# A two-layer decoder trunk on one core: other places for loads, for one quarter of a sum, for operands of the first pair and for the last additions

## The chip, the cores and the metric

The kernel runs on one core of one Trainium2 chip. The core has five engines with queues of their own: TensorE (PE; its weight loads are listed as PEld), VectorE (DVE), ScalarE (ACT), GpSimd (POOL) and SyncE (SP). SP, ACT and POOL also issue DMAs. The metric is the time of one execution in device microseconds (us), the median of the runs. Lower is better.

## The reference

All arithmetic is in float32, for 512 tokens of width 1024 and two layers:

```python
def rms_norm(x, gain):
    inv = lax.rsqrt(jnp.mean(x * x, axis=-1, keepdims=True) + NORM_EPS)
    return (x * inv) * gain

def swiglu(h, w_gate, w_up, w_down):          # 1024 -> 2816 -> 1024
    return (jax.nn.silu(h @ w_gate) * (h @ w_up)) @ w_down

def reference(x, ...):
    for l in range(DEPTH):
        x = x + 0.5 * swiglu(rms_norm(x, ffn1_norm[l]), ffn1_wg[l], ffn1_wu[l], ffn1_wd[l])
        h = rms_norm(x, mix_norm[l])
        z = h @ w_in[l]                       # q, k, v and three parts of a short convolution
        attn_out = sliding_window_attention(q, k, v, attn_sink[l])
        conv_out = short_conv(conv_B, conv_C, conv_h, conv_w[l])
        x = x + jnp.concatenate([attn_out, conv_out], axis=-1) @ w_out[l]
        x = x + 0.5 * swiglu(rms_norm(x, ffn2_norm[l]), ffn2_wg[l], ffn2_wu[l], ffn2_wd[l])
    return rms_norm(x, final_norm)
```

## The kernel before, in words

**Precision.** Each operand is split in a high part (a cast by ACT, `wh`, `xh`) and a low part (the rest, a subtraction by DVE, `wl`, `xl`); `split` at L226 makes both. A product is three matmuls on PE: high by high, high by low, low by high.

**Layout.** Between the parts the sum x lies turned, channels on partitions, in eight tiles of 128 channels by 512 tokens. A feed-forward part runs through its stages in the order of `INNER`: two plain column blocks ("p") with their projection down ("d"), five pairs of column blocks ("w"), two shares of the down projection ("s") and a closing down projection of the last two blocks ("d", (9, 10)). The last part (`LAST`) ends in "e" instead and leaves its result with tokens on partitions.

**Seven products for eight.** A pair of column blocks, a share and the output projection of the mixing part multiply two-by-two block matrices with seven block products (`CHAINS`, steps 0 to 6). Their x-side operands are sums of blocks, b11, b21, t2, t3, t1, t4, b22, made by `Seven.make` with DVE additions and a split. Their weight sides a11, a12, s2, s3, s1, a22, s4 come from loads into ten raw tiles. In `need_split`, s2 is a DVE addition in place (L265), s4 another (L285), or a DMA that adds on its way. `winograd2` calls `norm.make` for the operands t1, t4 and b22 after steps 0, 1 and 2.

**Weights ahead.** `plan` lists all weight units in the order of use. `take_split` makes the split of a unit two units ahead (`SPLIT_AHEAD`), `need_raw` loads four units ahead (`LOAD_AHEAD`), all by SP's queue, into eight raw tiles. Loads that add to what has been loaded go by GpSimd's queue. So during the last share of a part the first units of the next part's weights are loaded already.

**Shares and their way back.** A share's results come out with tokens on partitions. `Apart` collects them in quarters (o, t): channel half o, token half t. `Apart.send` lets ACT lay the 16-bit halves apart (L141) and SP issue two transposing DMAs per quarter (L898). `Apart.back` lets ACT put a turned quarter together (two copies, L911) and DVE add it to x (two additions, L915). A quarter that was not sent is turned by PE (L921) and added at L926. In the second share of `INNER`, quarters (0,0), (1,1) and (1,0) are sent after steps 3, 4 and 5 (`SENT_AT`), and (1,1) is taken back after step 6. In the closing projection, whose output blocks c come in the order 4, 5, 6, 7, 0, 1, 2, 3, `BACK_AT` takes (0,0) and (0,1) back after c = 4 and (1,0) after c = 5. Each block is added to x (L1250), and `Norm.take` and `Norm.square` make the next part's operands from it: `xh` (ACT, L458), `xl` (DVE, L459) and squares (L464, L467, L468).

**Order.** A scheduler sets the order on each engine from the order of the code and its own estimates; `tc.issue_after(i)` puts what is traced in it behind instruction i on i's engine. The opening and the last block of the end are written out by hand (`tc.manual_schedule`).

**Opening.** x is loaded in pieces (`load_x(tp, c0, n)`: token pair tp, n channel tiles from c0) by SP and ACT, beside the first weights; PE runs spin products on zeros (`spin`) until they land, then turns x (`turn_x`) and begins the first three groups.

**End.** `Finale.last` finishes four token tiles. `close` adds the last product to y (DVE) and sums the squares (ACT); `guess` takes a reciprocal root (ACT), `mend` improves it by a Newton step (DVE, L433 to L435), `scale` multiplies and stores. For the last tile the columns come in two halves of 256, `one` and `two`.

Of the kernel before, what the change touches and what calls it, by code (L numbers as in the profile page):

```python
# [49 lines left out]


SENT_AT = {3: (0, 0), 4: (1, 1), 5: (1, 0)}
BACK_AT = {4: ((0, 0), (0, 1)), 5: ((1, 0),)}
FINAL_AT = {4: (), 5: (4, 5)}
STREAM_BACK_AT = {9: 0, 11: 1, 16: 2, 18: 3}
SCORES_AT = (5, 6, 7, 8, 9, 10, 12, 13)
# [19 lines left out]
def trunk_kernel(  # L76
# [117 lines left out]
    order = []  # L194
    raw_of, split_of = {}, {}
    roomy = set()
    state = {"raw": 0, "split": 0, "group": 0, "late": None}

    def add_unit(*unit):
        units.append(unit)  # L200
# [10 lines left out]
    def need_raw(u):  # L211

        while state["raw"] <= min(u, len(units) - 1):
            n = state["raw"]
            _, _, kc, _, wide = units[n][0]
            name, shape = f"raw_{n}", (P, kc, wide)
            r = form(name, F32, shape) if n in roomy else stock(name, shape=shape)
            if n >= OPEN:
                load(r, n, 0, kc)
            for more in units[n][1:]:  # L220
                nc.gpsimd.dma_start(out=r, in_=rows_of(*more), accum_op=ALU.add)  # L221
            raw_of[n] = r
            state["raw"] += 1
# [10 lines left out]
    def need_split(g):  # L234
        while state["split"] <= min(g, len(order) - 1):
# [1 line left out]
            u, what = order[n]  # L237
            far = what == "far"
            if what in (None, "far"):
                need_raw(u if far else u + LOAD_AHEAD)  # L240
                raw = raw_of.pop(u)
            elif isinstance(what, tuple) and what[0] == "end":

                _, what, h = what
                at = {"a11": 2, "s2": 2, "s3": 3, "s1": 3, "a12": 4, "a22": 5, "s4": 5}[what]
                need_raw(u + 3 * at + h + LOAD_AHEAD)
                raws = {name: u + 3 * i + h for i, name in enumerate(END_LOADS)}
                if what == "s2":
                    with tc.issue_after(state["rest"]):
                        nc.vector.tensor_add(raw_of[raws["a11"]], raw_of[raws["a11"]], raw_of[raws["s1"]])  # L250
                raw = raw_of[raws["a11" if what in ("s2", "s4") else what]]
            elif isinstance(what, tuple):

                what, h, how = what
                far = how == "far"
                last = {"a11": 0, "a12": 4, "s2": 2, "s3": 6, "s1": 2, "a22": 8, "s4": 4}[what]
                need_raw(u + h if far else u + max(last, 4) + h + LOAD_AHEAD)
                a11, s1, a12, s3, a22 = (raw_of.get(u + 2 * i + h) for i in range(5))
                if what == "s2":

                    late = state["late"] if h else None
                    if not state["late"] and how == "share":
                        late = state["rest"]
                    with tc.issue_after(late) if late else nullcontext():
                        nc.vector.tensor_add(a11, a11, s1)  # L265
                raw = {"a11": a11, "a12": a12, "s2": a11, "s3": s3, "s1": s1, "a22": a22, "s4": a12}[what]
# [3 lines left out]
            if far:  # L270
                sent = split_far(hi, lo, raw)
            else:
                state["cast"], state["rest"] = (i.ins for i in split(hi, lo, raw))
            if isinstance(order[n][1], tuple) and order[n][1][0] == "end":
                if what == "a12":
                    nc.gpsimd.dma_start(out=raw_of[raws["a11"]], in_=raw, accum_op=ALU.add)
# [81 lines left out]
    def plan():  # L358
# [19 lines left out]
        def ffn(wg, wu, wd, stages, near=False):  # L378
            for what, b in stages:
# [3 lines left out]
                if what == "w":  # L383
                    seven(
                        lambda o, j, h: ((wg, wu)[o], KC // 2 * j + 2 * h, 2, 2 * b * P, S),
                        lambda what, h: "far" if (b, what, h) == (1, "a11", 0) else None,
                    )
                if what == "s":
                    seven(
# [2 lines left out]
                    )  # L392
                if what == "d":
                    cols(wd, 2 * b[0], 2 * len(b), KC, how, len(b) == 2)
                if what == "e":
                    u = len(units)
                    roomy.update(range(u, u + 3))
# [235 lines left out]
    nc.vector.memset(warm, 0.0)  # L633
    nc.scalar.activation(warm, warm, AF.Abs_reciprocal_sqrt, bias=eps)
# [243 lines left out]
    class Apart:  # L878
# [14 lines left out]
        def send(self, o, t):  # L893

            to = self.sent[o, t] = g8(f"turned_{self.name}_{o}_{t}", U16, (P, 2, NT, H))
            for u in range(2):
                halves = lay_apart(self.y[2 * t + u, o], f"{self.name}_{o}_{2 * t + u}")
                nc.sync.dma_start_transpose(  # L898
                    to.rearrange("p a c s -> p (a c) s")[:, :, u * P : (u + 1) * P],
                    halves.rearrange("p a n -> p (a n)"),  # L900
                )

        def back(self, o, t):

# [27 lines left out]
    def ffn(norm, stages, after=None, late=None):  # L932
# [39 lines left out]
        def winograd2(b, between=None):  # L972
# [12 lines left out]
            for step, (acc, operand, start) in enumerate(CHAINS):  # L985
# [195 lines left out]
        for i, (what, b) in enumerate(stages):  # L1181
# [34 lines left out]
            elif what == "s":  # L1216

                def between(step):
# [21 lines left out]
            for c, acc in down(rhs, b == (0,), final):  # L1240
# [19 lines left out]
    class Finale:  # L1260
# [49 lines left out]
        def add(self, t, o, acc, by):  # L1310
            part = self.y[t][o]
            nc.vector.scalar_tensor_tensor(part, acc, by, part, op0=ALU.mult, op1=ALU.add)

        def close(self, acc, t, half, by, ssq, c0=0):

            wide = acc.shape[1]
            y = self.y[t][half][:, c0 : c0 + wide]
            nc.vector.scalar_tensor_tensor(y, acc, by, y, op0=ALU.mult, op1=ALU.add)
            sq = work.tile([P, S], F32, tag="nsq", bufs=2, name=f"ysq_{half}_{t}_{c0}")
            nc.scalar.activation(sq[:, :wide], y, AF.Square, accum_out=ssq)  # L1320

        def guess(self, t, ssq, rest):
            r = small(f"r_end{t}", 1)
            nc.scalar.activation(r, ssq, AF.Abs_reciprocal_sqrt, scale=1.0 / D, bias=rest)
            return r

        def mend(self, t, ssq, rest, r):
            v, y = (small(f"{n}_end{t}", 1) for n in "vy")
            nc.vector.scalar_tensor_tensor(v, ssq, 1.0 / D, rest, op0=ALU.mult, op1=ALU.add)
            newton(y, r, v)  # L1330
            return y

        def root(self, t, ssq, rest):

            return self.mend(t, ssq, rest, self.guess(t, ssq, rest))

        def last(self, ops, accs):

# [397 lines left out]
```

## Time and profile before

| | us |
|---|---|
| median of 3 runs | 1630.61 |
| lowest and highest run | 1630.34, 1632.09 |
| the profiled execution: its own time | 1632.9 |
| the profiled execution: span from first to last instruction | 1631.1 |
| PE busy | 1616.7 (99%) |
| DVE busy | 1368.8 (84%) |
| ACT busy | 1178.1 (72%) |
| HBM read | 264.29 MB, 163 GB/s over the span |

The rows of the profile below give a start and a length in us, the engine (with q: its queue, where DMAs are issued), the line, the operation, what is written and read, and the size. In brackets stands how long the engine was idle before it and what ended that. One product of 512 columns shows as 0.39 us long, but the next starts while it runs.

### The profile page before, as it was taken

To read this page: it belongs to the slowest core of one execution; us is meant where nothing else is said; L and a number is where in the kernel's file an instruction comes from. 1 tells how busy PE (TensorE), PEld (TensorE's weight loads), DVE (VectorE), ACT (ScalarE), POOL (GpSimd) and SP (SyncE) were. 2 spreads that over 40 slices of the span, in tenths; PEclk is the share of its full clock that TensorE was granted. 3 is DMA by queue.
4 is the path that set the end of the run, shared out by engine and by line. 5 is a ranking of instruction groups with operands and counts; after the bars stand their busy time and mean duration, and the time that the engine had idled before them with its cause. 6 is when DMAs were issued, how large, how long until landed. Compare 5 with 4: busy or idle time off the path is not lost.

```text
span 1631.1 us, 21176 instructions
## 1 busy us (share of the span) xinstructions
PE 1616.7 (99%) x7572; PEld 1348.1 (83%) x7572; DVE 1368.8 (84%) x1779; ACT 1178.1 (72%) x1510; POOL 223.6 (14%) x199
## 2 busy tenths in 40 slices
PE   9999999999999999999999999999999999999998
PEld 6788888878898888888888888888788988888887
DVE  7978797888899977797999777989788998677997
ACT  6667777867766577778865777787586767878665
POOL 1211111001121111111011111110012111111121
PEclk9999999999999999999999999999999999999999
DMA  9899989922597698999967999999135978999992
GB/s 271 198 237 212 210 210 239 242 68 73 129 238 180 178 217 213 214 213 247 228 143 188 217 215 219 214 237 221 52 91 152 233 152 215 225 220 231 240 250 71
DMA packets 307166, 318.12 MB, mean 195 GB/s; under 512 B 125612, under 2 KB 188660, under 8 KB 307060
## 3 DMA queue, kind: packets, MB, share of 16 engines
q1 hardware_dynamic: 265140, 230.63, 49.9%
q0 software_dynamic: 41200, 85.47, 30.5%
q8 instruction: 59, 0.97, 0.2%
q10 hardware_dynamic: 720, 0.66, 0.1%
q14 instruction: 47, 0.39, 0.1%
HBM read 264.29 MB, written 2.10 MB: 163 GB/s over the span
## 4 chain that ended last, share of the span: by engine, by line
PE 91%; DVE 5%; ACT 2%; DMA 1%; issue 1%; SPq 0%; ACTq 0%; DVEq 0%
PE x L824 26%; PE y L824 13%; PE x_s L824 9%; PE w L824 6%; PE acc L313 6%; PE acc L312 6%; PE acc L315 6%; PE y_s L824 5%; PE w_s L824 3%; PE x_m L809 3%; PE y_m L809 1%; DVE wl L226 1%; PE y_e L824 1%; PE acc L686 1%; PE x_e L824 1%
## 5 line engine op out<-in xcount | busy, mean ns | idle before, releaser
L226 DVE TENSOR_TENSOR wl<-raw,wh 128x1024 fp32r<-128x1024 f32 (+1 forms) x493 | 599.6, 1224 | 171.8 <-ACT wh L226 171.0
L226 ACT CAST wh<-raw 128x1024 fp32r<-128x1024 f32 (+1 forms) x493 | 513.9, 1046 | 302.2 <-PE x L824 95.0
L313 PE MATMUL acc<-xl,wh 128*128 128x512 f32 x392 | 153.6, 392 | 2.8 <-DVE xl L459 2.8
L312 PE MATMUL acc<-xh,wh 128*128 128x512 f32 x392 | 153.4, 393 | 0.5 <-ACT wh L226 0.5
L315 PE MATMUL acc<-xh,wl 128*128 128x512 f32 x384 | 149.6, 390 | 0.0
L221 POOL DMA_DIRECT2D raw<-in_ffn_wu_dram x40 | 50.2, 1264 | 386.1 <-DVE wl L226 203.8
L313 PEld LDWEIGHTS acc<-xl,wh 128*128 128x128 f32 x392 | 73.7, 188 | 18.7 <-DVE xl L459 4.4
L312 PEld LDWEIGHTS acc<-xh,wh 128*128 128x128 f32 x392 | 73.7, 188 | 15.5 <-ACT wh L226 0.6
L315 PEld LDWEIGHTS acc<-xh,wl 128*128 128x128 f32 x384 | 72.1, 188 | 15.0
L221 POOL DMA_DIRECT2D raw<-in_ffn_wg_dram x40 | 49.4, 1261 | 200.9 <-DMA raw<-in_ffn_wu_dram 82.9
L221 POOL DMA_DIRECT2D raw<-in_ffn_wd_dram x34 | 41.0, 1206 | 246.3 <-DMA raw<-in_ffn_wd_dram 109.7
L265 DVE TENSOR_TENSOR raw<-raw,raw 128x1024 f32<-128x1024 f32 x58 | 70.6, 1221 | 3.6 <-DMA raw<-in_ffn_wu_dram 3.2
L1086 ACT COPY raw_a<-turned 128x1024 uint16<-128x1024 uint16 x48 | 63.5, 1357 | 0.0
L824 PE MATMUL x<-wl,ft2h 128*128 128x512 f32 x160 | 62.2, 390 | 1.1 <-DVE wl L226 1.1
L824 PE MATMUL y<-wh,ft4h 128*128 128x512 f32 x160 | 62.4, 390 | 0.1
L824 PE MATMUL w<-wh,fb21h 128*128 128x512 f32 x160 | 62.3, 390 | 0.0
L824 PE MATMUL y<-wh,ft3h 128*128 128x512 f32 x160 | 62.3, 390 | 0.0
L824 PE MATMUL w<-wl,fb21h 128*128 128x512 f32 x160 | 62.3, 389 | 0.0
L824 PE MATMUL x<-wh,ft2h 128*128 128x512 f32 x160 | 62.3, 389 | 0.0
L824 PE MATMUL x<-wh,ft1h 128*128 128x512 f32 x160 | 62.3, 389 | 0.0
L824 PE MATMUL x<-wh,ft2l 128*128 128x512 f32 x160 | 62.3, 389 | 0.0
L824 PE MATMUL x<-wh,ft1l 128*128 128x512 f32 x160 | 62.3, 389 | 0.0
(506 smaller groups left out, 4545.2 us busy)
## 6 DMA issues: line engine op xcount, KB each, us to landing
raw<-in_ffn_wu_dram SPq DMA_DIRECT2D x127, 512.0 KB, 5.4
raw<-in_ffn_wd_dram SPq DMA_DIRECT2D x105, 512.0 KB, 5.8
raw<-in_ffn_wg_dram SPq DMA_DIRECT2D x86, 512.0 KB, 5.3
raw<-in_ffn_wu_dram POOLq DMA_DIRECT2D x40, 512.0 KB, 8.9
raw<-in_ffn_wg_dram POOLq DMA_DIRECT2D x40, 512.0 KB, 6.2
raw<-in_w_in_dram SPq DMA_DIRECT2D x36, 512.0 KB, 4.0
raw<-in_ffn_wd_dram POOLq DMA_DIRECT2D x34, 512.0 KB, 9.4
raw<-raw POOLq DMA_DIRECT2D x21, 512.0 KB, 7.9
```

The costliest lines, as they stand in the source:

```text
L221: nc.gpsimd.dma_start(out=r, in_=rows_of(*more), accum_op=ALU.add)
L226: return nc.scalar.copy(hi, raw), eng.tensor_sub(lo, raw, f32(hi))
L265: nc.vector.tensor_add(a11, a11, s1)
L312: nc.tensor.matmul(acc, hi[:, k, :], rhs[k][0], start=k == first, stop=False)
L313: nc.tensor.matmul(acc, hi[:, k, :], rhs[k][1], start=False, stop=False)
L315: nc.tensor.matmul(acc, lo[:, k, :], rhs[k][0], start=False, stop=k == last)
L686: nc.tensor.matmul(opening[n], (lo if part == "w" else hi)[:, k, :], xl if part == "x" else xh, start=n not in begun, stop=k == KC - 1 and ...
L809: nc.tensor.matmul(accs[c // 2][:, c % 2, :], w[:, k, cols], x_[:, 2 * h + k, :], start=start and c % 2 == 0 and h + k + i == 0, stop=h + ...
L824: nc.tensor.matmul(accs[u], x_[:, 2 * h + k, tok], w[:, k, :], start=start and h + k + i == 0, stop=h + k == 2 and i == 2, skip_group_chec ...
L1086: nc.scalar.copy(words(raws[self.b][:, c, :]), self.to[:, :, c, :])
```

## The change

Six edits:

1. **Loads held.** After step 0 of the second share, `need_raw` stops at the last unit of the closing projection (`closing`, `state["hold"]`). After c = 5 of the closing projection the hold is lifted, and the loads of the next part are put behind the last transposing DMA of the share on SP's queue (`state["behind"] = apart.last`), until c = 0.
2. **First quarter.** (0,0) is taken back after step 6 of the second share, ahead of (1,1), not after c = 4.
3. **First part's pairs.** In the first feed-forward part t1, t4 and b22 are made a step later, behind the latest weight split.
4. **Second pair of the first part.** The second addition for s2 is put behind the first split of a12.
5. **Opening.** Two spin products fall away; the piece (1, 1, 1) of x goes third on ACT's queue, and (0, 2, 2) goes on SP's.
6. **End.** For the last token tile the additions of both halves come ahead of what waits for the first half's squares, and the Newton step of the last root is written with one dependent step less.

On the engines this gives: PE runs the same products (the two spin products less), in four places of the first pair in another order; DVE, ACT and SP run the same number of instructions in another order; GpSimd's order is unchanged.

```diff
-BACK_AT = {4: ((0, 0), (0, 1)), 5: ((1, 0),)}
+BACK_AT = {4: ((0, 1),), 5: ((1, 0),)}
...
             if n >= OPEN:
-                load(r, n, 0, kc)
+                with tc.issue_after(state["behind"]) if state["behind"] else nullcontext():
+                    load(r, n, 0, kc)
...
-                need_raw(u if far else u + LOAD_AHEAD)
+                need_raw(u if far else max(u, min(u + LOAD_AHEAD, state["hold"] or len(units))))
...
+                    if how == "behind":
+                        late = state["mark"]
                     with tc.issue_after(late) if late else nullcontext():
                         nc.vector.tensor_add(a11, a11, s1)
...
+                if isinstance(order[n][1], tuple) and order[n][1][2] == "mark":
+                    state["mark"] = state["rest"]
...
-                        lambda what, h: "far" if (b, what, h) == (1, "a11", 0) else None,
+                        lambda what, h: "far"
+                        if (b, what, h) == (1, "a11", 0)
+                        else {("a12", 0): "mark", ("s2", 1): "behind"}.get((what, h))
+                        if near and b == 3
+                        else None,
...
                     cols(wd, 2 * b[0], 2 * len(b), KC, how, len(b) == 2)
+                    if len(b) == 2:
+                        closing.append(len(units) - 1)
...
-    load_x(0, 2, 2, nc.scalar)
-    load_x(1, 1, 1)
+    load_x(1, 1, 1, nc.scalar)
+    load_x(0, 2, 2)
...
         turn_rows(0)
-        spin(2)
         turn_x(0)
...
-                nc.sync.dma_start_transpose(
+                self.last = nc.sync.dma_start_transpose(
...
-                if step < 3:
-                    norm.make(CHAINS[step + 4][1])
+                due = step + (4 if norm.i else 3)
+                if 3 < due < len(CHAINS):
+                    with nullcontext() if norm.i else tc.issue_after(state["rest"]):
+                        norm.make(CHAINS[due][1])
...
+                    if step == 0:
+                        state["hold"] = closing[norm.i // 3 * 2 + norm.i % 3 // 2]
                     if step == 6:
+                        apart.back(0, 0)
                         apart.back(1, 1)
...
                 if final:
+                    if c == 5:
+                        state["hold"], state["behind"] = None, apart.last
+                    if c == 0:
+                        state["behind"] = None
...
                 early = self.guess(a, ssq, done[:, a : a + 1])
-                by = self.mend(a, ssq, done[:, a : a + 1], early)
+                v = self.mean(a, ssq, done[:, a : a + 1])
+                one = self.total(products(psum("mm", [P, H], "z_0"), 1, 0, H, True), b, 0, 0.5)
+                by = self.mend(a, v, early)
+                ssq = small("ssq_end_0", 1)
+                self.squared(one, ssq, "one")
                 for late in (0, 1):
                     scale(a, by, late)
-                one = piece(products(psum("mm", [P, H], "z_0"), 1, 0, H, True), b, 0, 0.5)
+                two = self.total(products(psum("mm", [P, H], "z_1"), 1, H, H, True), b, 0, 0.5, H)
                 rest = done[:, b : b + 1]
                 nc.vector.scalar_tensor_tensor(
-                    rest, one, 1.0 / D, rest, op0=ALU.mult, op1=ALU.add
+                    rest, ssq, 1.0 / D, rest, op0=ALU.mult, op1=ALU.add
                 )
-                two = piece(products(psum("mm", [P, H], "z_1"), 1, H, H, True), b, 0, 0.5, H)
-                by = self.mend(b, two, rest, self.guess(b, two, rest))
+                half = small("half", 1)
+                nc.vector.tensor_scalar_mul(half, rest, -0.5)
+                ssq, v, by = (small(f"{n}_last", 1) for n in ("ssq", "v", "y"))
+                self.squared(two, ssq, "two")
+                r = self.guess(b, ssq, rest)
+                nc.vector.scalar_tensor_tensor(v, ssq, -0.5 / D, half, op0=ALU.mult, op1=ALU.add)
+                nc.vector.tensor_scalar(v, v, r, r, op0=ALU.mult, op1=ALU.mult)
+                nc.vector.scalar_tensor_tensor(by, v, 1.5, r, op0=ALU.add, op1=ALU.mult)
```

Here `total` is the addition of the old `close`, `squared` its sum of squares, and `mean` the first step of the old `mend`.

More of the change, by code (lines that the diff above doesn't have):

```diff
@@ L196, in trunk_kernel @@
     roomy = set()
-    state = {"raw": 0, "split": 0, "group": 0, "late": None}
+    state = {"raw": 0, "split": 0, "group": 0, "late": None, "hold": None, "behind": None}
+    closing = []
     def add_unit(*unit):
@@ L897, in send @@
                 halves = lay_apart(self.y[2 * t + u, o], f"{self.name}_{o}_{2 * t + u}")
-                nc.sync.dma_start_transpose(
+                self.last = nc.sync.dma_start_transpose(
                     to.rearrange("p a c s -> p (a c) s")[:, :, u * P : (u + 1) * P],
                     halves.rearrange("p a n -> p (a n)"),
-                )
+                ).ins
         def back(self, o, t):
@@ L1312, in add, with total, squared @@
             nc.vector.scalar_tensor_tensor(part, acc, by, part, op0=ALU.mult, op1=ALU.add)
-        def close(self, acc, t, half, by, ssq, c0=0):
[L1316 to L1320, printed above, removed]
+        def total(self, acc, t, half, by, c0=0):
+            y = self.y[t][half][:, c0 : c0 + acc.shape[1]]
+            nc.vector.scalar_tensor_tensor(y, acc, by, y, op0=ALU.mult, op1=ALU.add)
+            return y
+        def squared(self, y, ssq, name):
+            sq = work.tile([P, S], F32, tag="nsq", bufs=2, name=f"ysq_{name}")
+            nc.scalar.activation(sq[:, : y.shape[1]], y, AF.Square, accum_out=ssq)
+        def close(self, acc, t, half, by, ssq, c0=0):
+            self.squared(self.total(acc, t, half, by, c0), ssq, f"{half}_{t}_{c0}")
         def guess(self, t, ssq, rest):
@@ L1325, in guess, with mean, mend @@
             return r
-        def mend(self, t, ssq, rest, r):
-            v, y = (small(f"{n}_end{t}", 1) for n in "vy")
+        def mean(self, t, ssq, rest):
+            v = small(f"v_end{t}", 1)
             nc.vector.scalar_tensor_tensor(v, ssq, 1.0 / D, rest, op0=ALU.mult, op1=ALU.add)
+            return v
+        def mend(self, t, v, r):
+            y = small(f"y_end{t}", 1)
             newton(y, r, v)
@@ L1333, in root @@
         def root(self, t, ssq, rest):
-            return self.mend(t, ssq, rest, self.guess(t, ssq, rest))
+            early = self.guess(t, ssq, rest)
+            return self.mend(t, self.mean(t, ssq, rest), early)
         def last(self, ops, accs):
```

## The prediction

> **What bounds the kernel now.** I read the page first, then what TensorE (PE) waited for, then the instructions in order of time at those places.
>
> ```profile
> span 1631.1 us, 21176 instructions
> PE 1616.7 (99%) x7572; PEld 1348.1 (83%) x7572; DVE 1368.8 (84%) x1779; ACT 1178.1 (72%) x1510; POOL 223.6 (14%) x199
> ```
>
> PE is busy for 99% of the span. A change that leaves PE's products alone, as this one does, can only win the time in which PE stood, at most 14.4 us. The waits of PE name who held it; the first figure is the total in us:
>
> ```profile
> PE acc L313 <- DVE xl L459: 2.8, 4, 1.1
> PE xt L652 <- DMA xin<-in_x_dram: 1.6, 1, 1.6
> ...
> PE x L824 <- DVE wl L226: 1.1, 1, 1.1
> ```
>
> Ends of products are modelled, so I price a stall by starts: 340.06 to 340.29 in the rows below is the undisturbed pace, 0.23 us a product.
>
> ```profile
> 56.73 0.39 PE L824 MATMUL x<-wh,ft2l 128*128 128x512 f32 x1
> ...
> 58.53 0.39 PE L824 MATMUL x<-wh,ft2h 128*128 128x512 f32 x1
> ...
> 68.98 0.39 PE L824 MATMUL x<-wh,ft1l 128*128 128x512 f32 x1
> ...
> 69.76 0.40 PE L824 MATMUL y<-wh,ft4l 128*128 128x512 f32 x1
> ...
> 340.06 0.40 PE L315 MATMUL acc<-xh,wl 128*128 128x512 f32 x1
> 340.29 0.40 PE L312 MATMUL acc<-xh,wh 128*128 128x512 f32 x1
> ...
> 343.35 0.39 PE L315 MATMUL acc<-xh,wl 128*128 128x512 f32 x1
> ...
> 1145.01 0.39 PE L315 MATMUL acc<-xh,wl 128*128 128x512 f32 x1
> ...
> 1148.60 0.40 PE L315 MATMUL acc<-xh,wl 128*128 128x512 f32 x1
> ```
>
> First pair of column blocks: 56.73 to 58.53 is two steps, 1.80 - 0.46 = 1.34 lost; 68.98 to 69.76 two steps, 0.32 lost; together 1.66. Entry of the mixing stage, layer 0: five steps in 3.06, 1.92 lost. Layer 1: six steps in 3.59, 2.21 lost. With the 1.58 us at 6.93 (below) and the tail after the last product these are the places the change touches.
>
> **The change part by part.** *Loads held back and first quarter sooner (three feed-forward ends).* Three like stretches, each from the closing projection into the next stage's first group; the columns are length, then busy time of PE, PEld, DVE, ACT:
>
> ```profile
> 320.00:343.00 23.00, 21.65 (x95) 17.27 (x93) 22.95 (x34) 17.96 (x24) 0.00 (x0) 1.00 0.57 159
> 802.50:825.50 23.00, 23.00 (x103) 19.07 (x102) 21.82 (x32) 16.98 (x25) 0.00 (x0) 1.00 0.47 148
> 1125.00:1148.20 23.20, 21.83 (x94) 17.22 (x93) 22.84 (x34) 17.99 (x24) 0.00 (x0) 1.00 0.57 159
> ```
>
> The middle one runs the same code without a PE stall, and there VectorE (DVE) has 1.2 us to spare. At the other two DVE is full: it entered late.
>
> ```profile
> 311.62 1.05 ACT L226 CAST wh<-raw 128x1024 fp32r<-128x1024 f32 x1
> 316.17 2.57 ACT L911 COPY back<-turned 128x1024 uint16<-128x1024 uint16 x2 [3.50 <-DMA turned<-halves]
> ...
> 313.84 1.28 DVE L891 SCALAR_TENSOR_TENSOR apart<-x_s,apart 128x512 f32<-128x512 f32 x2
> 317.55 0.69 DVE L915 TENSOR_TENSOR x<-x,back 128x512 f32<-128x512 f32 x1 [2.43 <-ACT back L911]
> ...
> 319.68 1.23 DVE L226 TENSOR_TENSOR wl<-raw,wh 128x1024 fp32r<-128x1024 f32 x1 [0.21 <-ACT wh L226]
> 320.82 0.68 DVE L1250 SCALAR_TENSOR_TENSOR x<-acc,x 128x512 f32<-128x512 f32 x1
> 321.42 1.42 DVE L915 TENSOR_TENSOR x<-x,back 128x512 f32<-128x512 f32 x2
> ```
>
> ScalarE (ACT) stands 3.50 us for transposes that lie behind two 512 KB loads in SP's queue, and DVE 2.43 us behind ACT. The order of the changed program puts the copies and additions of quarter (0,0), whose transposes went out a step earlier, in these holes, ahead of quarter (1,1): two ACT copies, 2.57 us together as in the 316.17 row, from 312.6 to 315.1, and the two additions, until now 1.42 us at 321.42, at about 315.0 and 315.7. The copies of (1,1) then start at 315.1 if their transposes are there (1.1 us sooner), so the weight cast after them, DVE's 319.68 row and everything behind it come 1.1 earlier, and from the place of the 321.42 row on 1.1 + 1.3 = 2.4 earlier. For no stall the two late low parts must come sooner by what PE lost up to the second, 1.8. So both stalls go: 1.92 + 2.21 = 4.13, taken as 4.1. At the middle boundary the inserted copies push ACT later by about 1.8 and DVE by 0.4; 1.2 us of spare covers it: nothing.
>
> What is moved to do this: on SP's queue two loads of 512 KB per boundary go behind four transposes and two more behind the last two of them. Nothing changes on GpSimd's queue.
>
> ```profile
> raw<-in_w_in_dram SPq DMA_DIRECT2D x36, 512.0 KB, 4.0
> 319.93 2.79 SPq L209 DMA_DIRECT2D raw<-in_w_in_dram  x3
> 329.50 1.04 ACT L226 CAST wh<-raw 128x1024 fp32r<-128x1024 f32 x1
> ```
>
> The first of these loads feeds the cast at 329.50, wanted at about 327.1. The last transposes end before 319.93 even in the old order; 4.0 us (median to landing) gives 323.9, and with a queue in front 325.3. Cost zero, covered by 2 to 3 us; without that cover each us is a us of DVE. Bounds of the whole part: 4.14 at most; at least 2.6, if the (1,1) transposes land no sooner (then only the 1.3 us of additions is won, against 1.8 wanted: 0.5 to 0.8 stays at each entry).
>
> *First pair's operands.*
>
> ```profile
> 51.24 1.22 DVE L592 TENSOR_TENSOR hf<-hf 128x1024 f32<-128x1024 f32 x1
> ...
> 54.65 1.22 DVE L226 TENSOR_TENSOR ft1l<-hf,ft1h 128x1024 fp32r<-128x1024 f32 x1
> ...
> 56.92 1.22 DVE L226 TENSOR_TENSOR wl<-raw,wh 128x1024 fp32r<-128x1024 f32 x1
> ```
>
> PE waits at 56.96 for the low weights made at 56.92. DVE is back to back here, one wide instruction each 1.13 us. The new order takes the 51.24 and 54.65 rows from in front of it: 2.27 sooner, 54.65, done 55.87. In the new PE order the third product of the step wants it, one pace ahead of the 56.73 row, at 56.50. Gone: 1.34. What is late next: t1's two DVE steps and its cast now come behind the third product's weights, and counting on at 1.13 a row the low weights of the t1 product are done at 67.28, wanted two steps of 24 products (0.2265 each) after 56.50, at 67.37. That cover is 0.1 thin, so I leave 0.1 of stall: gain 1.55, between 0.8 (0.8 late there) and 1.66. In the next pair one addition goes behind a split on DVE; PE waits for nothing there, and the loads behind it start about 2 us sooner: zero.
>
> *First loads and two spin products less.*
>
> ```profile
> 1.19 2.74 PE L151 MATMUL idle<-zero 128*128 128x512 bf16 x6 [1.19 <-DVE warm L633]
> 4.08 0.61 PE L151 MATMUL idle<-zero 128*128 128x512 bf16 x2
> ...
> 6.93 0.44 PE L652 MATMUL xt<-ident,xin 128*128 128x128 f32 x2 [1.58 <-DMA xin<-in_x_dram]
> ...
> 5.64 0.40 ACT L226 CAST wh<-raw 128x256 fp32r<-128x256 f32 x1 [1.28 <-DMA raw<-in_ffn_wg_dram]
> ...
> 8.46 0.42 ACT L226 CAST wh<-raw 128x256 fp32r<-128x256 f32 x1
> ```
>
> The x piece awaited at 6.93 is issued third on ACT's queue instead of fourth on SP's, ahead of 256 KB that went first. Then the first weight piece (5.64) leads, and after it the second weight piece, whose issue does not move: it followed the first by 1.56 us, so its cast could stand at 5.64 + 1.56 = 7.2 at the soonest against 8.46. Gain between -0.3 (the small piece delays the first weights) and 0.9; nearest is the 8.46 row, which had 0.46 of other ACT work in front and goes to 7.9 or 8.0. I take 0.55; PE then works without holes to 27.9, so it lasts.
> The clock is a risk: six spins take 2.74 us, 0.43 each, and the pair at 4.08 starts the second in 0.22. So PE was at full pace by 4.08, before the two that go. The Trainium skill, "TensorE: Matmul & The Clock Gate", Part 1, says that PE runs at half clock until a free-running window of about 3.4 us was busy, at a moment that varies by run. The two rows agree with half pace first; by that rule fewer spins could leave the opening cold, a rival below.
>
> *Last additions.*
>
> ```profile
> 1623.91 0.28 PE L1415 MATMUL z<-wl,fb_e 128*128 128x256 f32 x1
> 1623.71 0.42 DVE L1318 SCALAR_TENSOR_TENSOR ytok<-z,ytok 128x256 f32<-128x256 f32 x1
> ...
> 1624.78 0.42 DVE L1318 SCALAR_TENSOR_TENSOR ytok<-z,ytok 128x256 f32<-128x256 f32 x1
> ...
> 1626.10 0.16 DVE L433 TENSOR_TENSOR y_end<-r_end 128x1 f32<-128x1 f32 x1 [0.17 <-ACT r_end L1324]
> ...
> 1626.68 0.75 DVE L1364 SCALAR_TENSOR_TENSOR ytok<-ytok,y_end,gain 128x512 f32<-128x512 f32 x1
> ```
>
> The last product ends at 1624.19, but the last addition starts at 1624.78, because the sum of squares of the other half is waited for between. Now it starts at 1624.25: 0.53. After the root two dependent steps follow instead of three: 0.19 (1626.10 to 1626.68 is three). The extra small step lies beside ACT's squares. Sum 0.7, bounds 0.2 (order only in part) and 0.75.
>
> **Sum.** 4.1 + 1.55 + 0.55 + 0.7 = 6.9. The profiled execution took 1632.9, 2.3 above the median 1630.61 of the runs: 1626.0 by its own time, 1623.7 by the median.
>
> **Rivals.**
> 1. The transposes land no sooner: 0.5 + 0.8 stays at the entries, and 0.2 more of late weights: gain 5.4, 1625.2. Against it: the SP order no longer has the two loads in front.
> 2. Given back: PE enters mixing 2 us sooner, and there ACT and DVE set the pace of attention, so 2 us come back in each layer: gain 2.9, 1627.7. For it: DVE is 84% busy over all. Against it: DVE enters as much sooner, and the middle boundary goes on without a stall.
> 3. Cold opening: the 12 products and 12 transposes before 11.1 at half pace cost 12 x 0.2 + 12 x 0.1 = 3.6, of which about 1 fits in PE's holes: loss 2.6 for a gain of 0.55; 1626.9.
> 4. Slower: the held-back weights come late. A cast that stands blocks ACT, its split DVE, and PE's low parts queue behind. It decides when the first load lands after about 331, 11 us after the 319.93 row: then each of three boundaries loses over 2.3 us, 6.9 in all; at 332.5 it gives 1630.6 - 6.9 + 3 x 3.8 = 1635. Against it: 4.0 us to landing.
> 5. The change does not do what it says, 1630.6: only if the late steps stay late in the new order; the programs' order speaks against it.
>
> **How the numbers follow.** Forecast 0.62, rivals 0.15, 0.10, 0.05, 0.05, 0.03. A measurement of this kernel tells about 0.2%, 3.3 us, from no change. Rival 2 lies near that edge and is halved; of rival 3 0.04 is faster. Faster 0.62 + 0.15 + 0.05 + 0.04 = 0.86, same 0.05 + 0.01 + 0.03 = 0.09, slower 0.05. The bounds of the parts give gains from 3.3 (2.6 + 0.8 - 0.3 + 0.2) to 7.45, so 1627.3 to 1623.2; with the runs' spread, 1622.4 to 1627.5. The likeliest case alone: 1622.7 to 1624.7.
>
> **What would show it.** Right: no PE wait for xl at the two entries, and the (0,0) copies on ACT between 312 and 316; no PE wait at 58; products of the opening about 0.6 us sooner; the last addition right behind the last product. Wrong: a PE or ACT wait for DMA of the next stage's weights, a new PE wait for wl in the t1 product, 0.43 us between products after 6 us, or new PE waits in attention.

## The result and the profile after

| | before | after |
|---|---|---|
| median of 11 runs each | 1632.09 | 1627.79 |
| lowest and highest run | 1629.66, 1638.06 | 1626.69, 1629.26 |
| the profiled execution: its own time | 1632.9 | 1627.75 |
| the profiled execution: span | 1631.1 | 1626.0 |

The ratio is 0.9966, with a 95% interval of 0.9956 to 0.9976: the changed kernel is faster by 0.34% (0.24 to 0.44%), 4.3 us by the medians. The forecast of "faster" came true. The forecast time of 1623.7 did not: the measured 1627.79 lies 0.3 us above the top of the range. Part of that isn't the change: before's median in these 11 runs is 1.5 us above that of the 3 runs known earlier. Counted as a gain, 4.3 us came of the 6.9 forecast, inside the 3.1 to 8.2 that the range allowed.

The page of the changed kernel begins as before's did, with 3 us less of span at a PE that is as busy:

```profile
span 1626.0 us, 21171 instructions
...
PE 1616.4 (99%) x7570; PEld 1350.2 (83%) x7570; DVE 1367.4 (84%) x1779; ACT 1177.3 (72%) x1510; POOL 223.6 (14%) x199
```

**The entries of the mixing stage.** Here and below, a kernel's profile is that of one execution; before and the kernel called base below have two each. Two stretches of the changed kernel, one around each entry; the columns are length, then busy time of PE, PEld, DVE, ACT:

```profile
312.00:345.00 33.00, 33.00 (x151) 27.39 (x150) 30.28 (x43) 26.32 (x33) 0.00 (x0) 1.00 0.67 190
1120.00:1148.00 28.00, 28.00 (x125) 23.18 (x124) 25.79 (x36) 21.23 (x29) 0.00 (x0) 1.00 0.63 185
```

PE does not stand; the 1.92 and 2.21 us of before are gone. ACT, whose copies waited 3.50 us for the transposes, now does all four without a break in front of them, where the prediction put them. The two of quarter (1,1) are the last of the four and start at about 314.7, against 316.17 before:

```profile
312.29 5.00 ACT L922 COPY back<-turned 128x1024 uint16<-128x1024 uint16 x4
```

**The first pair.** Starts of PE's products in the changed kernel, first where t2 begins to be used, then at t1:

```profile
57.49 0.39 PE L835 MATMUL x<-wh,ft2h 128*128 128x512 f32 x1
57.72 0.39 PE L835 MATMUL x<-wh,ft2l 128*128 128x512 f32 x1
57.94 0.39 PE L835 MATMUL x<-wl,ft2h 128*128 128x512 f32 x1
...
68.82 0.48 PE L835 MATMUL x<-wl,ft1h 128*128 128x512 f32 x1
69.14 0.39 PE L835 MATMUL x<-wh,ft1h 128*128 128x512 f32 x1
```

The 1.34 us are gone, and of the 0.32 at t1 0.09 stays (0.32 between the last two rows, for 0.23). That is 1.57.

**The opening.** PE of the changed kernel, then the same core's stretches of 3.41 us; in a stretch the figure after the five engines is the granted clock:

```profile
5.67 0.44 PE L664 MATMUL xt<-ident,xin 128*128 128x128 f32 x2 [0.64 <-DMA xin<-in_x_dram]
6.87 0.50 PE L698 MATMUL acc<-xh,wh 128*128 128x512 f32 x1 [0.77 <-ACT xh L470]
...
9.53 0.63 PE L698 MATMUL acc<-xh,wl 128*128 128x512 f32 x1
9.96 0.63 PE L698 MATMUL acc<-xl,wh 128*128 128x512 f32 x1
...
29.36 0.26 PE L180 MATMUL par_ps<-ident,rows 56*128 56x56 f32 x1
```

```profile
4.28:7.69 3.41, 1.95 (x11) 1.04 (x10) 1.26 (x3) 1.70 (x5) 0.00 (x0) 1.00 1.00 310
7.69:11.10 3.41, 3.41 (x13) 2.83 (x13) 1.75 (x3) 1.52 (x3) 0.00 (x0) 0.50 0.99 338
11.10:14.51 3.41, 3.29 (x14) 2.10 (x13) 2.42 (x4) 3.14 (x8) 0.00 (x0) 1.00 1.13 349
```

The piece of x that before awaited until 6.93 is there at 5.67, and the first product starts at 6.87, not 7.13. Then PE gets half of its clock from 7.69 to 11.10, and its products come 0.43 us apart (9.53 to 9.96). The small product that ends the opening in the list above, the second transposes of the gains, stood in before at

```profile
27.92 0.26 PE L180 MATMUL par_ps<-ident,rows 56*128 56x56 f32 x1
```

So in these two executions the opening lost 1.44 us. I call the start of this product the end of the opening from here on.

**The end.** DVE, PE and ACT of the changed kernel behind the last product:

```profile
1619.44 0.28 PE L1447 MATMUL z<-wl,fb_e 128*128 128x256 f32 x1
```

```profile
1619.76 0.42 DVE L1337 SCALAR_TENSOR_TENSOR ytok<-z,ytok 128x256 f32<-128x256 f32 x1 [0.41 <-PE z L1447]
...
1621.09 0.27 DVE L1481 TENSOR_SCALAR v_last<-v_last,r_end 128x1 f32<-128x1 f32 x1 [0.17 <-ACT r_end L1351]
1621.39 0.16 DVE L1482 SCALAR_TENSOR_TENSOR y_last<-v_last,r_end 128x1 f32<-128x1 f32 x1
1621.59 0.75 DVE L1396 SCALAR_TENSOR_TENSOR ytok<-ytok,y_last,gain 128x512 f32<-128x512 f32 x1
```

The last addition starts 0.32 us after the last product's start (0.87 before): 0.55 won. From it to the last scaling are 1.83 us (1.90 before): 0.07 won.

The sum of the two profiles: + 1.44 - 1.57 - 4.13 - 0.62 = -4.9, of -5.1 by the spans. Nothing is given back in attention: in the two profiles the last product of squares at the end of the mixing stage is ahead by 2.4 us in layer 0, and by 4.4 in layer 1, no less than the parts before it make (2.0 and 4.3). First before, then after:

```profile
505.10 0.48 PE L523 MATMUL ssq<-sql,ones_r 128*128 128x512 f32 x1
...
1309.56 0.50 PE L523 MATMUL ssq<-sql,ones_r 128*128 128x512 f32 x1
```

```profile
502.67 0.47 PE L535 MATMUL ssq<-sql,ones_r 128*128 128x512 f32 x1
...
1305.12 0.48 PE L535 MATMUL ssq<-sql,ones_r 128*128 128x512 f32 x1
```

### The profile page after: what moved, and what is told of

Same layout as the page of the kernel before. It is cut to its first block, busy times and chain, and to the rows that moved or that the text cites. A ratio compares the mean times of both kernels' runs of the same rounds, so it can differ in the third digit from the quotient of the medians.

```text
span 1626.0 us, 21171 instructions
## 1 busy us (share of the span) xinstructions
PE 1616.4 (99%) x7570; PEld 1350.2 (83%) x7570; DVE 1367.4 (84%) x1779; ACT 1177.3 (72%) x1510; POOL 223.6 (14%) x199
## 4 chain that ended last, share of the span: by engine, by line
PE 97%; DVE 1%; DMA 1%; ACT 0%; issue 0%; ACTq 0%; DVEq 0%
PE x L835 27%; PE y L835 13%; PE x_s L835 9%; PE acc L318 7%; PE acc L319 7%; PE acc L321 7%; PE w L835 7%; PE y_s L835 4%; PE x_m L820 3%; PE w_s L835 3%; PE y_m L820 1%; PE y_e L835 1%; PE acc L698 1%; PE x_e L835 1%; PE w_m L820 1%; DMA raw<-in_ffn_wd_dram 1%
## 5 line engine op out<-in xcount | busy, mean ns | idle before, releaser
L835 PE MATMUL x<-wl,ft1h 128*128 128x512 f32 x160 | 62.4, 390 | 0.0
L835 PE MATMUL w<-wh,fb21l 128*128 128x512 f32 x160 | 62.3, 389 | 0.0
```

Source lines behind the costliest of these rows:

```text
L835: nc.tensor.matmul(accs[u], x_[:, 2 * h + k, tok], w[:, k, :], start=start and h + k + i == 0, stop=h + k == 2 and i == 2, skip_group_chec ...
```

## The experiments

Three sets of four, each set on one chip beside runs of before. Medians in us; the last column is the ratio to before on the same chip with its 95% interval. "Base" is the changed kernel with the two spin products put back.

| run | what it is | median | lowest, highest | ratio to before |
|---|---|---|---|---|
| first chip | before, 18 runs | 1631.75 | 1628.24, 1637.52 | |
| e1_spins | base | 1626.26 | 1625.51, 1627.19 | 0.9959 (0.9943 to 0.9975) |
| e2_loads | after, old order of first loads | 1627.29 | 1625.76, 1629.88 | 0.9966 (0.9952 to 0.9980) |
| e3_opening | base, old order of first loads | 1626.28 | 1625.67, 1629.02 | 0.9966 (0.9950 to 0.9981) |
| e8_filled | base and six more spin products | 1626.27 | 1625.94, 1629.17 | 0.9964 (0.9950 to 0.9977) |
| second chip | before, 35 runs | 1632.19 | 1628.45, 1641.06 | |
| e4_nohold | base, loads not held | 1627.49 | 1625.97, 1633.79 | 0.9975 (0.9961 to 0.9989) |
| e5_back | base, (0,0) back after c = 4 | 1627.14 | 1625.35, 1630.12 | 0.9969 (0.9957 to 0.9981) |
| e6_neither | base without both | 1628.46 | 1626.67, 1633.87 | 0.9978 (0.9965 to 0.9990) |
| e7_pair | base, first pairs as before | 1627.94 | 1627.19, 1629.33 | 0.9969 (0.9959 to 0.9979) |
| third chip | before, 33 runs | 1630.45 | 1627.81, 1633.27 | |
| e9_end | base, end as before | 1626.52 | 1626.24, 1627.24 | 0.9980 (0.9971 to 0.9989) |
| e10_entries | before with edits 1 and 2 | 1628.82 | 1628.00, 1631.96 | 0.9994 (0.9985 to 1.0003) |
| e11_before | before once more, 8 runs | 1629.66 | 1627.76, 1632.62 | 0.9996 (0.9986 to 1.0006) |
| e12_spins_again | base | 1626.11 | 1625.35, 1630.17 | 0.9977 (0.9968 to 0.9986) |

The medians of the new kernels move little from chip to chip (base 1626.26 and 1626.11); before's move by 1.7 us, and its runs spread over 5 to 13 us. Since before's spread makes the ratios wide, I compare the new kernels by their medians, and the profiles by their rows. The changed kernel itself is in none of the three sets, and the second set has no base of its own. Distances from one set to another therefore carry a few tenths of doubt at the least; where a distance within a set exists, it is given too.

### The opening

The changed kernel with the two spin products back:

```diff
         turn_rows(0)
+        spin(2)
         turn_x(0)
```

> The changed kernel with the two spin products put back between the gains' transposes and the first x transposes; its new order of first loads stays. Theory A (the lost opening comes from the two spin products that went: TensorE then had too little work between 4.3 and 7.7 us, and the granted clock was 0.52 over 8.0 to 11.2): no half clock here, products 0.23 to 0.36 us apart after 8 us, the second transposes of the gains (29.36 us in the changed kernel, 27.92 before) at about 27.4, time 1627.8 - 2.0 = 1625.8. Rival B (the new order of loads makes it, by moving the waits of TensorE to 5.03 and 6.1 us): half clock here too, 1627.8. Rival C (the half clock is chance, in some executions of every kernel): half clock or not, the median moves by less than 0.5 us.

Without them, and with the old order of loads:

```diff
-    load_x(1, 1, 1, nc.scalar)
-    load_x(0, 2, 2)
+    load_x(0, 2, 2, nc.scalar)
+    load_x(1, 1, 1)
```

> The changed kernel with the old order of the first loads, still without the two spin products. Theory A (too few spin products): half clock over some 3.4 us of the opening as in the changed kernel, second transposes of the gains at 29.4 us or later (29.9 if the order of loads was worth its 0.55), time 1627.8 to 1628.3. Rival B (the order of loads makes the half clock): full clock, opening as before at 27.5 to 27.9, time 1626.4. Rival C (chance): within 0.5 us of 1627.8, with the clock either way.

Both of these edits together:

> The changed kernel with the whole opening of before: the two spin products and the old order of loads. Theory A and rival B alike: full clock in the opening, second transposes of the gains at 27.92 us as before, and the gain of the other three parts alone, 4.13 + 1.57 + 0.62 = 6.3 us from the median of before, 1632.1 - 6.3 = 1625.8; against the run with the two spin products alone this tells what the order of loads is worth (0.55 predicted). Rival C (chance): the same as the changed kernel, 1627.8.

And the base with PE's waits filled:

```diff
         turn_rows(0)
+        spin(2)
         turn_x(0)
+        spin(3)
...
+            if c == 1:
+                spin(3)
             go(0, c - 1, c, "hwx")
```

> The changed kernel with the two spin products back and six more of 0.22 us: three behind the first x transposes, three behind the second, where TensorE stood 0.64 and 0.77 us. Theory A (what counts is how much TensorE does in the stretch before): full clock throughout, time as the kernel with two spin products, 1625.8, or up to 0.3 more where a spin product stands in front of a transpose whose data has landed. If two spin products are not enough (half clock there), this one is the one at full clock and 2 us faster. Rival C (chance): no difference.

The stretches of the base (first fence) and of the kernel with the old loads and no spin products (second), each with the end of its opening:

```profile
4.05:7.46 3.41, 2.48 (x14) 1.60 (x14) 1.48 (x3) 2.01 (x5) 0.00 (x0) 1.00 0.96 281
7.46:10.87 3.41, 3.35 (x17) 2.14 (x17) 2.34 (x5) 2.83 (x6) 0.00 (x0) 1.00 1.00 319
```

```profile
27.34 0.26 PE L180 MATMUL par_ps<-ident,rows 56*128 56x56 f32 x1
```

```profile
5.78:9.19 3.41, 2.02 (x11) 1.23 (x11) 1.83 (x3) 2.38 (x5) 0.00 (x0) 1.00 1.03 311
9.19:12.60 3.41, 3.41 (x13) 2.70 (x12) 1.54 (x3) 1.84 (x4) 0.00 (x0) 0.50 1.04 351
```

```profile
29.54 0.26 PE L180 MATMUL par_ps<-ident,rows 56*128 56x56 f32 x1
```

The half clock goes with the spin products, not with the order of loads. Both profiles without them show 3.41 us at a granted clock of 0.50, under the new order and the old; none of the twelve profiles with them shows a fall back to half clock in the opening. In time, on one chip and with the old order, 1627.29 without them stands against 1626.28 with them, 1.0 us; from one set to another the base, 1626.26, is 1.5 below the changed kernel, with all its runs of this set but the highest below 1626.7, where the changed kernel's lowest lies. By the times the half clock isn't in every execution without them: four of the nine runs of e2_loads lie at 1625.8 to 1626.1, like the base.

The order of loads is worth nothing that shows: 1626.26 with the new, 1626.28 with the old. The end of the opening in profiles that show no such fall is 27.34, 27.57, 28.05, 27.46, 28.43, 27.71 and 27.74 with the new order (mean 27.76), 27.92, 27.68 and, in the second profile of before, 27.54 with the old (mean 27.71). Left out of these means is e10_entries, which starts late and is shown in the last section. Six more spin products bring nothing to the median; in their profile the opening ends at 28.54, later than in any of these.

### The entries of the mixing stage

Loads not held (on the base, as all that follow):

```diff
-                    if step == 0:
-                        state["hold"] = closing[norm.i // 3 * 2 + norm.i % 3 // 2]
...
-                    if c == 5:
-                        state["hold"], state["behind"] = None, apart.last
-                    if c == 0:
-                        state["behind"] = None
```

> The kernel of the run with the two spin products (median 1626.3, from here on the base), with the loads no longer held: SP issues the next stage's loads where before did, ahead of the last transposes; quarter (0,0) is still taken back after step 6. My theory (both edits are needed, the transposes land 1.1 us sooner without the loads in front, the additions give 1.3): only the additions are won, of 1.8 wanted, so 0.5 and 0.8 us of stall stay at the two entries of the mixing stage: 1627.6. Rival (the transposes land no sooner for the hold, all of the gain is the copies and additions moved up): 1626.3, no stall. Rival (all of it is the hold): 4.1 slower, 1630.4.

First quarter back where it was:

```diff
-BACK_AT = {4: ((0, 1),), 5: ((1, 0),)}
+BACK_AT = {4: ((0, 0), (0, 1)), 5: ((1, 0),)}
...
-                        apart.back(0, 0)
```

> The base with quarter (0,0) taken back after c = 4 as before; the loads stay held. My theory: the transposes of (1,1) come 1.1 us sooner, but the two copies and two additions stand again behind them, so of the 1.8 us wanted 1.1 is won: 0.8 and 1.1 us of stall stay at the entries: 1628.2. Rival (all of the gain is the hold): 1626.3, no stall at the entries. Rival (all of it is the earlier quarter): stalls of 1.92 and 2.21 as before, 1630.4.

Both of these together:

> The base with both edits at the ends of the feed-forward parts undone. My theory: stalls of 1.92 and 2.21 us at 340 and 1145 us as before, 1626.3 + 4.1 = 1630.4. Rival (given back later: attention set the pace anyway, and the entries were worth less than their stalls): between 1627 and 1629.5 with the same stalls. Beyond this, before's runs spread over 1628 to 1637 us and the base's over 1625.5 to 1627.2: if the spread comes from the transposes' wait at these entries, it is back here.

Before with edits 1 and 2 alone, and before once more:

> Before with edits 1 and 2 alone (held loads, first quarter sooner). Prediction: 4.1 us faster than before, about 1628.0 beside a before of 1632.1, and no stall at either entry of the mixing stage. Rival, by the last runs (both edits undone cost 2.2, and the profiled execution of that kernel showed no stall at the first entry): 1630.0; the stalls of before's one profile are then larger than those of most executions.

> Before once more, for a second look. If the stalls at the two entries of the mixing stage belong to the order of the work, they stand here again with 1.9 and 2.2 us; if they hang on when the transposes land in one execution, at least one of them differs by over 0.5. The opening: full clock from 8 us on, as in the first look, or half clock over 3.4 us if the two spin products are not enough in every execution.

The second profile of before (e11_before) decides how this is read. Its stretches at the two entries:

```profile
320.00:343.00 23.00, 23.00 (x103) 19.07 (x102) 22.05 (x33) 17.47 (x25) 0.00 (x0) 1.00 0.45 132
1122.00:1145.00 23.00, 23.00 (x103) 19.04 (x103) 21.31 (x32) 16.29 (x24) 0.00 (x0) 1.00 0.41 119
```

PE does not stand at either: the 4.13 us that I priced are not in this execution of the same kernel, whose own time is 1627.76. What differs are the transposes. The view of their line gives SP's time for one (least, median, most, in ns) and how long the copies waited for them. In this order they are the first profile of before, the second, e6_neither, e4_nohold, e5_back, and the changed kernel:

```profile
L898 SPq DMA_TRANSPOSE turned<-halves x18: 1311/2828/5466, 296.8 to 1123.6; - x18
...
  ACT back L911: 7.7, 4
```

```profile
L898 SPq DMA_TRANSPOSE turned<-halves x18: 1313/2567/3339, 295.0 to 1115.7; - x18
...
  ACT back L911: 1.2, 1
```

```profile
L910 SPq DMA_TRANSPOSE turned<-halves x18: 1245/2331/5622, 291.4 to 1119.2; - x18
...
  ACT back L923: 3.7, 2
```

```profile
L910 SPq DMA_TRANSPOSE turned<-halves x18: 1314/2630/5987, 292.8 to 1118.3; - x18
...
  ACT back L923: 3.2, 2
```

```profile
L910 SPq DMA_TRANSPOSE turned<-halves x18: 1231/1340/4434, 293.3 to 1114.9; - x18
```

```profile
L909 SPq DMA_TRANSPOSE turned<-halves x18: 1232/1322/5577, 295.2 to 1114.7; - x18
```

In the four profiles in which the loads aren't held, the median transpose holds SP for 2.3 to 2.8 us, and ACT's copies wait for 1.2 to 7.7 us in all, by execution. In the ten in which they are held it is 1.3 us in seven and 1.7 to 2.1 in three (e8_filled, e7_pair, e3_opening), and in none of the ten do the copies wait for a transpose or PE for `xl` at an entry. One of the ten is e5_back, so holding the loads takes the wait away by itself: with the quarter at its old place, PE is busy throughout at both entries:

```profile
318.00:341.00 23.00, 23.00 (x103) 19.03 (x102) 21.41 (x31) 16.34 (x24) 0.00 (x0) 1.00 0.64 189
1122.00:1145.00 23.00, 23.00 (x103) 19.06 (x102) 21.64 (x32) 16.34 (x24) 0.00 (x0) 1.00 0.67 199
```

With the quarter moved but the loads not held (e4_nohold) the first entry is clean, and at the second PE waits 0.6 in all:

```profile
PE acc L319 <- DVE xl L471: 0.6, 2, 0.3
```

In the profile of e6_neither the same row says 1.4 in all, at the second entry alone. Since a kernel without either edit can stall for 4.13, 1.4 or 0, one profile of e4_nohold doesn't show what the moved quarter is worth alone. In time, both edits are worth 2.2 us by the median (1628.46 against 1626.26, from one set to another), half of what I had; within the second set e4_nohold lies 1.0 and e5_back 1.3 below e6_neither, with runs that overlap. Alone, on before, they give 1.6 us (1628.82 against 1630.45), but only 0.8 against the eight runs of e11_before, and the interval of the ratio reaches 1. Their other effect may be on the spread: the highest runs of e4_nohold and e6_neither lie 6.3 and 5.4 us above their medians, those of the nine kernels that hold the loads 0.7 to 4.1. Against it stands before on the third chip, with 2.8 and 3.0. The 0.9 of e5_back against the base is not explained by the entries; part of it may be the chip. Its profile lost 1.2 us at 776 us, where a weight's low part came late in the second share; the profiles of e3_opening and e8_filled have the same wait, those of the base do not. What makes it come and go wasn't tried.

### The first pair and the end

First pairs as before:

```diff
-                due = step + (4 if norm.i else 3)
-                if 3 < due < len(CHAINS):
-                    with nullcontext() if norm.i else tc.issue_after(state["rest"]):
-                        norm.make(CHAINS[due][1])
+                if step < 3:
+                    norm.make(CHAINS[step + 4][1])
...
-                        else {("a12", 0): "mark", ("s2", 1): "behind"}.get((what, h))
-                        if near and b == 3
```

> The base with the operands of the first pairs made as before (edits 3 and 4 undone). My theory: stalls of 1.34 and 0.32 us at 57 and 69 us as before, 1626.3 + 1.55 = 1627.8. Rival (the stall only moves to the waits of the next loads or weights): less than 0.5 slower. If before's spread of 1628 to 1637 comes from here, it is back.

```profile
PE x L834 <- DVE wl L228: 1.1, 1, 1.1
```

The wait is back in the list of waits, and the median is 1627.94, 1.7 us above the base of the other sets (1.55 expected). The spread stays under 2.2 us: before's doesn't come from here alone.

End as before (`close` for both halves, `mend` with its three steps at the last root):

> The base (the changed kernel with the two spin products) with the end of before: the last addition waits again for the other half's squares, and the last root has its three dependent steps. The changed kernel's profile gives 0.55 for the addition (0.32 us behind the start of the last product, 0.87 before) and 0.07 for the steps (1.83 us from the addition to the last scaling, 1.90 before), not the 0.19 of the prediction: so 0.62 slower, 1626.9. By the prediction's term: 0.7, 1627.0. Rival (the stores that follow set the end): less than 0.2.

1626.52 against 1626.11 on the same chip: 0.4 slower, of 0.62 by the rows, and inside the base's own spread. The base again:

> The base once more beside these: 1626.3 again and a spread of under 2 us; full clock in the opening (no slice under 1.00 after 8 us). If the half clock still comes in some executions at the two spin products, this look shows it or a run or two lie 1.5 to 2 us above the rest.

1626.11 with full clock behind the first 7 us in its profile, but a spread of 4.8 us, against the under 2 expected: two of eleven runs lie at 1628.7 and 1630.2. No version here is faster than the base, which lies 1.5 to 1.7 us below the changed kernel (in other sets), and 5.5 and 4.3 below before on the two chips where both ran; e3_opening and e8_filled are level with it.

## Why the prediction was right and wrong

**The sum by its own time held but for one term.** The prediction put 1632.9 - 6.9 = 1626.0 for an execution like the profiled one. The base, which has the two spin products back, has medians of 1626.26 and 1626.11. Term by term: first pair 1.57 by rows and 1.7 by the run, for 1.55; end 0.62 by rows and 0.4 by the run, for 0.7; entries 4.13 in the two profiles, for 4.1. That the total agrees to 0.3 us is partly luck: the 0.55 for the opening is in 1626.0 and not in the base, and a median of one kernel is set beside one execution of another.

**The opening had the wrong sign**, 1.44 lost for 0.55 won. Two steps failed. The first: "So PE was at full pace by 4.08, before the two that go." From this the prediction took it that the two could go at no cost in clock. In ten of the twelve profiles that have them they are still at half pace, as in e3_opening:

```profile
4.08 1.03 PE L151 MATMUL idle<-zero 128*128 128x512 bf16 x2
```

And full pace, once reached, wasn't kept: the changed kernel had it from 4.28 on and lost it at 7.69. In the stretch before the half clock PE was busy for 1.95 and 2.02 of 3.41 us, against 2.48 in the base; that this shorter busy time is what brings the half clock is likely but not shown, since 1.83 us were enough in the first profile of before (last section). Rival 3 had the half pace right, but not its course or its price. It let PE stay cold until 11.1; in fact PE was at full pace and fell back for one stretch. Its loss of 2.6 (from 12 products and 12 transposes, where the rows of before have 11 and 10) compares with the 1.7 between the end of the opening at half clock (29.36, 29.54) and without it (27.7 to 27.8 in the mean). Its gain of 3.7 lies nearer to the measured 4.3 than the forecast's 6.9, but by two errors that cancel: the loss here too high, and the gain at the entries too. The Trainium skill, "TensorE: Matmul & The Clock Gate", Part 1, gives the window of about 3.4 us and says that its phase differs by run: the traces agree, with 3.41 us at 0.50 and a full pace that begins at 4.1 to 10.5 us. It puts the return to half clock after an idle window; here a window that was 57% busy was enough.

The second step that failed is the order of loads: taken as 0.55 from the place of the second weight cast, it is worth nothing that shows. The small piece of x came 1.3 us sooner and the first product only 0.26, as it then waited 0.77 for ACT's `xh`.

**The step from the profile to the median failed.** "1626.0 by its own time, 1623.7 by the median" takes the 2.3 us by which the profiled execution was above the median as a constant beside the gain. It was part of the gain: the stalls of 4.13 us are those of a long execution, and a short one of the same kernel (1627.76) has none. If that holds for other executions, of which there are only these two profiles, a gain that removes the stalls lowers the long ones by 4.1 and the short ones by nothing; by the median it is 1.6 to 2.2, so 1.9 to 2.5 was too much. The opening's 2.0 comes on top. Together that is 3.9 to 4.5, but the sum can't be closed better than before's median holds still: from 1623.7 to 1627.79 it is 4.1, and from the gain forecast to the gain measured it is 2.6.

**How the entries were won was half right.** ACT's wait for transposes behind the loads in SP's queue was the cause, as the prediction said. That 1.1 us of it would go by the hold and the rest by the moved quarter was not borne out: with the hold alone (e5_back) no stall stays, where this split leaves 0.8 and 1.1. SP spent 1.3 us on the median transpose for 2.8 before. Rival 1, for which the transposes land no sooner, falls, as in none of the ten profiles with the hold do the copies wait for one. Rival 4 falls too: in the changed kernel no engine waits for a held weight at an entry. Rival 2 falls by the rows of the last squares, and rival 5 by the result.

## What to carry to other kernels

Before a stall is priced from one profile, see whether that execution is a long or a short one of its kernel: a stall that waits for a DMA may be what makes it long, and then the gain is counted from its own time, not from the median. Spin products are not only a bridge to the first data: here taking two of them away was followed by 3.4 us at half clock in both profiles, at a cost of 1.0 to 1.5 us. Busy time alone didn't foretell it, so price such a removal with several executions. DMAs that an engine waits for go ahead of bulk loads in their queue; here the wait was gone in all ten profiles in which they did.

## What the runs showed of the hardware that was not expected

- A stretch of 3.41 us in which PE was busy for 1.95 (in e2_loads 2.02) us was followed by one at a granted clock of 0.50; the first stretch at full pace of the other profiles but one, with 2.36 us or more, was not. Busy time alone doesn't decide it: in the first profile of before the stretch had 1.83 us, with the two spin products in it, and the clock stayed at 1.00. What else decides it stays open:

```profile
4.13:7.54 3.41, 1.83 (x13) 1.33 (x13) 1.18 (x2) 1.30 (x4) 0.00 (x0) 1.00 0.96 287
```

- The first half pace ends anywhere from 4.1 to 10.5 us after the start, for the same first instructions. In the profile of e10_entries, which has the two spin products, products were still 0.42 us apart behind 8.5 us, and the opening ended at 29.74 for 27.7. So the two spin products don't keep every opening from this loss. The granted clock in the stretches there reads 1.00, so early in a trace the pace is to be read from starts:

```profile
8.51 0.63 PE L696 MATMUL acc<-xh,wl 128*128 128x512 f32 x1
8.93 0.63 PE L696 MATMUL acc<-xl,wh 128*128 128x512 f32 x1
...
10.57 0.40 PE L696 MATMUL acc<-xh,wl 128*128 128x512 f32 x1
10.80 0.40 PE L696 MATMUL acc<-xl,wh 128*128 128x512 f32 x1
```

- A transposing DMA held SP's queue for 2.3 to 2.8 us in the median in the profiles where loads lie between, and for 1.3 to 2.1 where they are held.
- On DVE a one-column step that takes two scalars from memory (L1481) is 0.27 us long where its neighbours, without such scalars, are 0.16; so the last root's step less won 0.07, not 0.19.
